# Six of the eight chunks of the output projection moved into the retention stage, their partial sums kept in DRAM

## The chip, the cores and the metric

The kernel runs on one core of one Trainium2 chip. The metric is the device time of one execution in microseconds (us), the median of three runs. All times of instructions come from one profiled execution, counted from the start of its span.

## What is computed

Two layers over 768 tokens (512 latent tokens and 256 context tokens), width 1024, all in float32. Each layer projects the normed input once, feeds the columns to three groups of heads, joins their outputs, multiplies by `w_out`, and then runs a squared-ReLU channel mixer. Cut to what matters here:

```python
def trunk_layer(...):
    h = rmsnorm(x, norm_g[0]) * (1 + sc1) + sh1
    qa, ka, va, qr, kr, vr, gr, z, xbc, dt = split(h @ w_in)
    att = attention_mixer(...)        # 6 heads of 64: features 0..383
    ret = retention_mixer(...)        # 4 heads of 64: features 384..639
    ssd = ssd_mixer(...)              # 6 heads of 64: features 640..1023
    o = concatenate([att, ret, ssd]) @ w_out
    x = x + g1 * rmsnorm(o, norm_g[1])
    h2 = rmsnorm(x, norm_g[2]) * (1 + sc2) + sh2
    x = x + g2 * rmsnorm(square(relu(h2 @ w_ff1)) @ w_ff2, norm_g[3])
```

The context stream goes through the same steps in layer 0 and is not needed after the mixers of layer 1. So layer 0 handles six tiles of 128 tokens, layer 1 four. The adaLN terms (`sh`, `sc`, `g`) are products of two conditioning vectors with `w_mod`, in 12 sections of 512 columns a layer.

## The kernel before

**Products.** A float32 operand is split into two parts, high and low, and every large product is three matmuls (`mm3`, L465): high by high, high by low and low by high. A weight unit (`wunit`, L210) is loaded raw by SP's queue into one of three buffers `wr` (512 KB each), the high part is made by ACT (L221) and the low part by DVE (L222, or POOL), into one of three buffers `wh` and `wl`.

**Order.** The program is written as one stream of instructions; a scheduler at build time gives every engine and SP's queue a fixed order from it. An instruction that stands earlier in the text goes first when both are ready, one that is not ready in the scheduler's reckoning is overtaken. At run time each engine works through its own list in order, and so does SP's queue. Generators are interleaved by hand: `run(gen, n)` takes `n` steps.

**The mixers** (`mixers`, L501) end with attention and retention. While the six attention heads run (L1127), one step of `fill` is taken after each pair of query tiles, three pairs a head in layer 0 and two in layer 1. `fill` (L1124) holds 12 steps in layer 0 and 10 in layer 1 that project the retention's keys, values, queries and gates, and in layer 0 then 24 steps that compute modulation sections 4 to 9: sections 4 and 5 split (`mod_split`), sections 6 to 9 as plain float32 products (`mod_whole`, L320, whose matmul is L325). In layer 0 what is left of `fill` is taken in the retention, five steps at a time.

**Retention** (L1143 to L1161) has four heads. A head transposes its keys and queries (`ret_prep`, L999), multiplies scores (`rs`, L1035) and chunk sums (`rd`, L1039), runs a chain of ten small DVE steps for the states (L1050, L1052), multiplies the outputs (`ry`, L1056 and L1057), and norms them on ACT and DVE (L1064 to L1074). After heads 1 and 3 the finished pair is transposed into chunk 3 and chunk 4 of `mixT` (`put_tok`, L1107; the high part on ACT, L1101, the low part on DVE, L1103). Chunks 0 to 2 (attention) and 5 to 7 (state-space) are put there as well, by `puts`, in heads 0 to 2. The POOL engine multiplies `kw` (L1006) and the gains (L1086, L1087) and makes the low part of chunks 0 to 2 (L1103).

**The output projection** (`wout_phase`, L1192) takes 8 chunks by 2 halves of 512 columns by 3 matmuls for each tile of tokens: 48 matmuls of 128x512. The first six products of tile 0 (18 matmuls) are issued in head 3 of the retention (`wout_begin`, L1180), the rest after it. The chunks go in this order, those of the retention last:

```python
WO_ORDER = [5, 6, 7, 0, 1, 2, 3, 4]
```

Its weights are four units, each four chunks by 512 columns.

**After each tile** `sandwich` (L1219) takes the two halves out of PSUM: ACT squares them (L1230), DVE multiplies them by the gate row (L1232), a root gives the factor, DVE adds the residual (L1236), the sum is stored, and `norm_tile` (L451) norms it again: square (L428), root, scale (L454), eight transposes on PE (`nps`), modulation on DVE and ACT (L445, L443), high part (L448), low part (L449). Its scratch `tt` (`t` in the code, later `xh`) and `xt` have two buffers each; `tt` is in use from the gate multiply to L449. Beside the last tile PE runs the first products of the channel mixer (`ff_begin`, L1253) on tokens whose norm is done; then the channel mixer goes on and needs the last tile's high part first.

**Memory.** The mixers' pool is closed before the pool of the output stage is opened, and the latter may lie in the memory of the former.

## Time and profile before

| | |
|---|---|
| three runs | 1888.5, 1886.2, 1888.09 us |
| median | 1888.09 us |
| profiled execution: span from its first to its last instruction | 1880.8 us |
| PE busy | 1753.1 us, 93% |
| DVE busy | 1219.7 us, 65% |
| ACT busy | 703.0 us, 37% |
| POOL busy | 369.1 us, 20% |
| moved by DMA | 217.00 MB, mean 115 GB/s |

The profile gives the span of the profiled execution; a time of its own beside that span was not recorded. The median of the runs is 7.3 us above the span. PE is TensorE, PEld its weight loads, which run beside the matmuls. A matmul's recorded time reaches over the next one's start, so the step from one start to the next says what it costs PE. PEclk is the granted clock as a share of 2.4 GHz. In a row of the timeline, what stands in brackets is the idle time before the instruction and what ended it.

### The profile page before, as it was taken

Reading aid. Unit: us, or ns where it says so; the run is one execution under the profiler, and the core shown is the slowest. Engines: PE = TensorE matmul, PEld = TensorE weight load, DVE = VectorE, ACT = ScalarE, POOL = GpSimd, SP = SyncE. Lnnn points to the kernel's source line nnn. Section 1 sums busy time; section 2 is a strip of 40 time slices with the busy share of each in tenths; the row PEclk is TensorE's granted clock in tenths of the full one; section 3 lists DMA queues with packets and bytes.
Section 4 is the critical chain, followed back from the end, with each engine's and each line's share of the span. In section 5 each row is a group of like instructions: output and inputs, shape, how many; then the busy total and the mean of one; then the engine's idle time right before and its main releaser. Section 6 shows DMA issues by size and latency. Waiting matters only on the chain. (4 is left out here: it accounts for less than half of the span.)

```text
span 1880.8 us, 24641 instructions
## 1 busy us (share of the span) xinstructions
PE 1753.1 (93%) x8991; PEld 1443.0 (77%) x8991; DVE 1219.7 (65%) x2462; ACT 703.0 (37%) x1267; POOL 369.1 (20%) x391
## 2 busy tenths in 40 slices
PE   6987999997999999999999979888987999999998
PEld 2877977655878888888888868777866788888886
DVE  5868985664668566566566586788876654444445
ACT  5543376652461111201201275433772532222222
POOL 0047232313001100100100132553022021111112
PEclk9999999997999999999999999999996999999999
DMA  8410243366444334434434433224324432222332
GB/s 274 124 52 32 89 149 104 104 182 184 146 135 136 124 101 132 125 107 123 126 105 118 152 123 91 65 71 124 100 73 110 147 122 90 90 90 91 102 105 95
DMA packets 189078, 217.00 MB, mean 115 GB/s; under 512 B 67667, under 2 KB 142237, under 8 KB 188957
## 3 DMA queue, kind: packets, MB, share of 16 engines
q1 hardware_dynamic: 188956, 215.43, 37.8%
q8 instruction: 71, 1.16, 0.2%
q14 instruction: 51, 0.41, 0.1%
HBM read 189.66 MB, written 25.72 MB: 115 GB/s over the span
## 5 line engine op out<-in xcount | busy, mean ns | idle before, releaser
L467 PE MATMUL f<-h_h,wh_f 128*128 128x512 f32 (+1 forms) x800 | 280.3, 351 | 1.4 <-ACT h_h L448 1.4
L469 PE MATMUL f<-h_h,wl_f 128*128 128x512 f32 (+1 forms) x800 | 281.0, 352 | 0.0
L468 PE MATMUL f<-h_l,wh_f 128*128 128x512 f32 (+1 forms) x800 | 280.1, 350 | 0.8 <-DVE h_l L449 0.8
L1299 POOL TENSOR_TENSOR r<-r 128x768 f32<-128x768 f32 (+1 forms) x64 | 93.8, 1466 | 847.4 <-ACT r L1298 837.8
L467 PE MATMUL f<-wh_g,uh 128*128 128x512 f32 x640 | 253.0, 396 | 4.1 <-DVE acc L1327 1.7
L468 PE MATMUL f<-wl_g,uh 128*128 128x512 f32 x640 | 252.6, 395 | 0.0
L469 PE MATMUL f<-wh_g,ul 128*128 128x512 f32 x640 | 251.8, 394 | 0.0
L221 ACT ACTIVATE wh_f<-wr_f 128x1024 fp32r<-128x1024 f32 x64 | 66.5, 1055 | 377.2 <-PE f L469 164.4
L1329 DVE TENSOR_TENSOR acc<-acc,f 128x512 f32<-128x512 f32 x140 | 96.0, 686 | 121.0 <-PE f L469 119.6
L467 PEld LDWEIGHTS f<-h_h,wh_f 128*128 128x128 f32 x800 | 152.0, 190 | 23.0 <-ACT h_h L448 1.5
L468 PEld LDWEIGHTS f<-h_l,wh_f 128*128 128x128 f32 x800 | 151.1, 189 | 22.8 <-DVE h_l L449 1.0
L469 PEld LDWEIGHTS f<-h_h,wl_f 128*128 128x128 f32 x800 | 151.2, 189 | 20.8
L405 DVE SCALAR_TENSOR_TENSOR ga<-wr_mg,cg_a,ga 128x512 f32<-128x512 f32 x216 | 153.6, 762 | 14.6 <-DMA wr_mg<-in_w_mod_dram 14.6
L467 PEld LDWEIGHTS f<-wh_g,uh 128*128 128x128 f32 x640 | 120.1, 188 | 33.5 <-DVE acc L1327 2.2
L469 PEld LDWEIGHTS f<-wh_g,ul 128*128 128x128 f32 x640 | 120.1, 188 | 28.8
L468 PEld LDWEIGHTS f<-wl_g,uh 128*128 128x128 f32 x640 | 120.2, 188 | 27.4 <-DVE wl_g L222 0.2
L1298 ACT ACTIVATE r<-f 128x768 f32<-128x768 f32 (+1 forms) x64 | 44.8, 699 | 193.4 <-PE f L469 133.4
L1300 DVE CAST uh<-r 128x768 fp32r<-128x768 f32 (+1 forms) x64 | 32.3, 505 | 123.2 <-POOL r L1299 123.2
L222 DVE TENSOR_TENSOR wl_f<-wr_f,wh_f 128x1024 fp32r<-128x1024 f32 x64 | 77.6, 1220 | 51.3 <-ACT wh_f L221 51.3
L222 DVE TENSOR_TENSOR wl_g<-wr_g,wh_g 128x1024 fp32r<-128x1024 f32 x62 | 76.6, 1241 | 50.9 <-ACT wh_g L221 50.8
L221 ACT ACTIVATE wh_g<-wr_g 128x1024 fp32r<-128x1024 f32 x64 | 67.3, 1056 | 94.2 <-DMA wr_g<-in_w_ff_dram 53.6
L467 PE MATMUL xbc<-h_h,wh_xbc 128*128 128x512 f32 (+1 forms) x208 | 73.5, 353 | 7.7 <-ACT cin L692 7.7
(405 smaller groups left out, 3774.3 us busy)
## 6 DMA issues: line engine op xcount, KB each, us to landing
wr_f<-in_w_ff_dram SPq DMA_DIRECT2D x64, 512.0 KB, 3.7
wr_g<-in_w_ff_dram SPq DMA_DIRECT2D x64, 512.0 KB, 3.5
wr_mg<-in_w_mod_dram SPq DMA_DIRECT2D x192, 128.0 KB, 2.9
wr_m<-in_w_mod_dram SPq DMA_DIRECT2D x24, 512.0 KB, 3.8
m<-in_w_mod_dram SPq DMA_DIRECT2D x32, 256.0 KB, 4.2
wr_o<-in_w_out_dram SPq DMA_DIRECT2D x16, 512.0 KB, 4.1
wr_xbc<-in_w_in_dram SPq DMA_DIRECT2D x14, 512.0 KB, 5.3
xmid<-xt SPq DMA_DIRECT2D x10, 512.0 KB, 2.6
```

Source lines behind the costliest of these rows:

```text
L221: S.activation(hv[:, a0 : a0 + an], r, AF.Copy)
L222: (lo_eng or V).tensor_tensor(lv[:, a0 : a0 + an], r, hv[:, a0 : a0 + an].bitcast(F32), ALU.subtract)
L405: V.scalar_tensor_tensor(acc[:, s], r2[:, k % 2], w, acc[:, s], ALU.mult, ALU.add)
L467: T.matmul(o, a[0], b[0], start=first, stop=False)
L468: T.matmul(o, a[0], b[1], start=False, stop=False)
L469: T.matmul(o, a[1], b[0], start=False, stop=last)
L1298: S.activation(r, q[:, :NT], AF.Relu)
L1299: G.tensor_tensor(r, r, r, ALU.mult)
L1300: V.tensor_copy(uh, r)
L1329: V.tensor_tensor(acc[tt][:, ns], acc[tt][:, ns], qs[tt][half], ALU.add)
```

## The change

The attention loop takes five steps of `fill` a time in heads 4 and 5, and whatever is left is taken before the retention begins. `wout_begin` now loads three units of two chunks each (chunks 5 and 6, 7 and 0, 1 and 2, all 1024 columns), with the six `puts` in between, ahead of head 0. Then it runs six chunks for every tile and half as a step-wise generator, two steps after each step of a head: a half is 18 matmuls into a PSUM bank, a copy by ACT into a staging buffer, and a store of 256 KB to the DRAM tensor `opd`. A half is two steps, so there are 24 steps in layer 0 and 16 in layer 1. `wout_phase` loads one unit (chunks 3 and 4), runs 12 matmuls a tile, and `sandwich` loads the tile's row block of `opd` into `t`, adds the two halves of PSUM to it on DVE, and goes on from there; the gate multiply moves from DVE to POOL, but for the last tile. Lines of comment that the change takes out are left away here.

```diff
             for _ in att_head(h):
-                run(fill, 1)
+                run(fill, 1 if h < 4 else 5)
+        run(fill)
         mixT = alloc_mix()
...
-        puts = [lambda j=j: put_ssd(j) for j in range(3)] + [lambda j=j: put_att(j) for j in range(3)]
-        wpre = None
-        wo = iter(())
+        wo = wout_begin(l, mixT, stage, [lambda j=j: put_ssd(j) for j in range(3)] + [lambda j=j: put_att(j) for j in range(3)])
+        next(wo)
         for h in range(4):
-            if h == (3, 2)[l] and l in (0,1,):
-                wpre = wout_units(l, (0,))
-            if h == (3, 3)[l] and wpre:
-                wo = wout_begin(l, mixT, wpre, 6)
             if h < 3:
                 ret_decay(h + 1)
                 ret_prep(h + 1)
                 centre_v(h + 1)
             for i, _ in enumerate(ret_head(h)):
-                run(fill, 5)
                 if i == 1:
                     ret_gain(h)
-                if i in (0,2) and puts:
-                    puts.pop(0)()
                 run(wo, 2)
-        run(fill)
         run(wo)
...
+    WO_FIRST = ((5, 6), (7, 0), (1, 2))
+    WO_LAST = (3, 4)
+    opd = [dp.tile([TOK, D], F32, name=f"opd{l}") for l in range(DEPTH)]
+    def wout_unit(l, ks):
+        src = lambda a0, an: [(krows(w_out[l], ks[a0], 1, 0, D), 0, D)]
+        return wunit(src, (128, 2, D), f"o{l}{ks[0]}")
...
+    def wout_begin(l, mixT, stage, puts):
+        NQ = 6 if l < DEPTH - 1 else 4
+        us = []
+        for n, ks in enumerate(WO_FIRST):
+            us.append(wout_unit(l, ks))
+            for _ in ks:
+                puts.pop(0)()
+        yield
+        for tt in range(NQ):
+            cols = slice(tt * 128, (tt + 1) * 128)
+            for half in range(2):
+                q = pB([128, 512], f"ob{l}{tt}{half}")
+                for u, ks in enumerate(WO_FIRST):
+                    for i, k in enumerate(ks):
+                        wout_part(mixT, us[u], q, i, k, cols, half, u + i == 0, u + i == 3)
+                    if u == 1:
+                        yield
+                o = stage(512, f"ob{tt}{half}")
+                S.activation(o, q, AF.Copy)
+                nc.sync.dma_start(rows(opd[l], tt)[:, half * 512 : (half + 1) * 512], o)
+                yield
     def wout_phase(l, cpool, mixT, h2T):
...
+        w = wout_unit(l, WO_LAST)
         for tt in range(NQ):
...
             for half in range(2):
-                d = done[half] if tt == 0 else 0
-                q.append(q0[half] if tt == 0 and q0[0] is not None else (pB, pC)[tt % 2]([128, 512], f"op{l}{half}{tt}"))
-                for i in range(d, KC):
-                    wout_part(mixT, us, q[half], half, WO_ORDER[i], cols, i == 0, i == KC - 1)
+                q.append((pB, pC)[tt % 2]([128, 512], f"op{l}{half}{tt}"))
+                for i, k in enumerate(WO_LAST):
+                    wout_part(mixT, w, q[half], i, k, cols, half, i == 0, i == 1)
...
-            sandwich(cpool, q, g1, x_in(l, tt), rows(xmid[l], tt), tt, l, 1, h2T, V, 2, pC if last else None)
+            sandwich(cpool, q, g1, x_in(l, tt), rows(xmid[l], tt), tt, l, 1, h2T, V, 2, pC if last else None, V if last else G, rows(opd[l], tt))
...
         hv = (slice(0, 512), slice(512, 1024))
+        if part is not None:
+            nc.sync.dma_start(t, part)
+            for j in range(2):
+                V.tensor_tensor(t[:, hv[j]], t[:, hv[j]], o[j], ALU.add)
+            o = [t[:, hv[j]] for j in range(2)]
         for j in range(2):
             S.activation(junk, o[j], AF.Square, accum_out=ss[:, j : j + 1])
```

## Rows read from the trace of the kernel before

**Rows 1.** The page: busy time of each engine.

```profile
PE 1753.1 (93%) x8991; PEld 1443.0 (77%) x8991; DVE 1219.7 (65%) x2462; ACT 703.0 (37%) x1267; POOL 369.1 (20%) x391
```

**Rows 2.** Busy time by stretch: PE, PEld, DVE, ACT, POOL, granted clock, DMA share, GB/s.

```profile
355.00:401.30 46.30, 43.62 (x225) 24.15 (x224) 31.97 (x73) 32.74 (x68) 13.80 (x7) 1.00 0.55 155
...
437.00:491.30 54.30, 44.71 (x250) 39.33 (x251) 36.12 (x94) 17.93 (x25) 13.11 (x12) 0.81 0.47 141
491.30:561.40 70.10, 67.60 (x318) 54.71 (x316) 45.16 (x110) 44.85 (x92) 0.00 (x0) 1.00 0.46 155
1411.60:1471.80 60.20, 48.22 (x242) 42.59 (x241) 40.32 (x132) 15.13 (x29) 13.96 (x14) 0.72 0.34 80
1471.80:1526.50 54.70, 52.50 (x303) 44.91 (x301) 35.72 (x76) 35.02 (x67) 6.62 (x2) 1.00 0.56 192
```

**Rows 3.** The same view, head 1 of layer 1's retention.

```profile
1425.00:1437.90 12.90, 10.84 (x54) 9.82 (x53) 9.17 (x35) 3.64 (x9) 2.72 (x3) 0.63 0.25 67
```

**Rows 4.** PE's timeline: outputs of one retention head in layer 0.

```profile
445.72 0.39 PE L1056 MATMUL ry<-vrr,W 128*128 128x64 f32 x2
445.95 0.39 PE L1057 MATMUL ry<-rst,q 128*128 128x64 f32 x2
...
447.88 0.64 PE L1056 MATMUL ry<-vrr,W 128*128 128x64 f32 x2
448.31 0.63 PE L1057 MATMUL ry<-rst,q 128*128 128x64 f32 x2
```

**Rows 5.** Granted clock around them, columns as in rows 2.

```profile
441.70:447.00 5.30, 2.76 (x24) 2.51 (x22) 3.70 (x10) 1.63 (x2) 3.52 (x3) 1.00 0.98 267
447.40:463.80 16.40, 10.24 (x47) 9.71 (x46) 11.84 (x32) 4.55 (x7) 5.36 (x5) 0.50 0.36 123
```

**Rows 6.** Groups of PE instructions, 401.3 to 491.3 us: busy, mean ns, idle before.

```profile
L325 PE MATMUL mq<-wr_m,csil 128*2 128x512 f32 x42 | 19.6, 592 | 2.2 <-DMA wr_m<-in_w_mod_dram 2.1
L1057 PE MATMUL ry<-rst,q 128*128 128x64 f32 x48 | 11.4, 327 | 8.7 <-DVE rst L1052 8.7
L467 PE MATMUL op<-wh_o,mix_h 128*128 128x512 f32 x24 | 9.8, 409 | 0.0
```

**Rows 7.** PE's timeline: the first and the last of 39 products in a row.

```profile
523.09 0.39 PE L467 MATMUL op<-wh_o,mix_h 128*128 128x512 f32 x1
...
531.87 0.39 PE L469 MATMUL op<-wh_o,mix_l 128*128 128x512 f32 x1
```

**Rows 8.** Last output of head 3 on PE, and chunk 4's low part on DVE.

```profile
482.81 0.39 PE L1057 MATMUL ry<-rst,q 128*128 128x64 f32 x2
...
490.36 0.96 DVE L1103 TENSOR_TENSOR mix_l<-sT,mix_h 128x768 fp32r<-128x768 f32 x1 [2.28 <-ACT mix_h L1101]
...
1464.65 0.39 PE L1057 MATMUL ry<-rst,q 128*128 128x64 f32 x2
...
1471.07 0.69 DVE L1103 TENSOR_TENSOR mix_l<-sT,mix_h 128x512 fp32r<-128x512 f32 x1 [1.63 <-ACT mix_h L1101]
```

**Rows 9.** Last tile of layer 0: second square (ACT) and low part (DVE), timeline.

```profile
546.88 0.58 ACT L1230 ACTIVATE junk<-op 128x512 f32<-128x512 f32 x1
...
561.34 1.23 DVE L449 TENSOR_TENSOR h_l<-tt,h_h 128x1024 fp32r<-128x1024 f32 x1 [1.69 <-ACT h_h L448]
```

**Rows 10.** Loads of `xt`: first issue in layer 0; time to landing, layer 0, then 1.

```profile
490.03 0.90 SPq L1223 DMA_DIRECT2D xt<-in_x_dram  x2
...
DMA to landing us min/median/max: 4.2/5.0/5.4
...
DMA to landing us min/median/max: 2.6/2.6/2.6
```

**Rows 11.** POOL's and DVE's timelines: a small DVE step beside POOL, and without it.

```profile
452.42 1.81 POOL L1103 TENSOR_TENSOR mix_l<-fa,mix_h 128x768 fp32r<-128x768 f32 x1 [1.52 <-ACT mix_h L1101]
...
453.02 1.23 DVE L1069 TENSOR_SCALAR var<-var 128x6 f32<-128x6 f32 x1
...
468.78 0.17 DVE L1069 TENSOR_SCALAR var<-var 128x6 f32<-128x6 f32 x1
```

More of the change, by code (lines that the diff above doesn't have):

```diff
@@ L1153, in mixers @@
             for i, _ in enumerate(ret_head(h)):
-                run(fill, 5)
                 if i == 1:
                     ret_gain(h)
-                if i in (0,2) and puts:
-                    puts.pop(0)()
                 run(wo, 2)
-        run(fill)
         run(wo)
-        return mixT, wpre
-    WO_ORDER = [5, 6, 7, 0, 1, 2, 3, 4]
-    def wout_unit(l, half, u, pool=None):
-        return wunit(wcols(w_out[l], 4 * u, [(half * 512, 0, 512)]), (128, 4, 512), f"o{l}{half}{u}", None, pool)
@@ L1170, in wout_units @@
-    def wout_units(l, halves):
-        us = {(half, u): wout_unit(l, half, u) for half in halves for u in ((1, 0) if half == 0 else (1,))}
-        return us, [None, None], [0, 0]
-    def wout_part(mixT, us, q, half, k, cols, first, last):
-        mh, ml = mixT
-        h, lo = us[half, k // 4]
-        mm3(q, (mh[:, k, cols], ml[:, k, cols]), (h[:, k % 4, :], lo[:, k % 4, :]), first, last)
-    def wout_begin(l, mixT, pre, n):
-        us, q, done = pre
-        for i in range(n):
-            half, j = divmod(i, 6)
-            if i == 0:
-                t = pA([128, 2, 512], f"op{l}0")
-                q[:] = [t[:, 0], t[:, 1]]
-            wout_part(mixT, us, q[half], half, WO_ORDER[j], slice(0, 128), j == 0, False)
-            done[half] = j + 1
-            yield
+        return mixT
@@ new lines, in tile_hybrid_backbone, with wout_part @@
+    WO_FIRST = ((5, 6), (7, 0), (1, 2))
[4 more added lines that the diff above has]
+        return wunit(src, (128, 2, D), f"o{l}{ks[0]}")
+    def wout_part(mixT, w, q, i, k, cols, half, first, last):
+        mh, ml = mixT
+        h, lo = w
+        ns = slice(half * 512, (half + 1) * 512)
+        mm3(q, (mh[:, k, cols], ml[:, k, cols]), (h[:, i, ns], lo[:, i, ns]), first, last)
@@ L1192, in wout_phase @@
     def wout_phase(l, cpool, mixT, h2T):
         NQ = 6 if l < DEPTH - 1 else 4
-        mixT, wpre = mixT
-        us, q0, done = wpre or ({}, [None, None], [0, 0])
-        for half in range(2):
-            for u in (1, 0):
-                if (half, u) not in us:
-                    us[half, u] = wout_unit(l, half, u, cpool if half == 1 and (u == 0 or l == 1) else None)
+        w = wout_unit(l, WO_LAST)
         for tt in range(NQ):
@@ L1217, in wout_phase, with sandwich @@
         return pre
-    def sandwich(pool, o, gate, xsrc, xdst, tt, nl, nwhich, hT, eng, bufs=2, half_bank=None, geng=None):
+    def sandwich(pool, o, gate, xsrc, xdst, tt, nl, nwhich, hT, eng, bufs=2, half_bank=None, geng=None, part=None):
         xt = pool.tile([128, D], F32, tag="xt", name="xt", bufs=bufs)
@@ L1425, in tile_hybrid_backbone @@
         mixT = mixers(0, mp, hT, lambda: big(pa, "mix0"), kvw)
-    dump("mix0", mixT[0][0].bitcast(F32))
+    dump("mix0", mixT[0].bitcast(F32))
     R = ExitStack()
@@ L1441, in tile_hybrid_backbone @@
         mixT = mixers(1, mp, hT, lambda: big(pr, "mix1", SEQ), kvw)
-    dump("mix1", mixT[0][0].bitcast(F32))
+    dump("mix1", mixT[0].bitcast(F32))
     L = ExitStack()
```

## The prediction

> **What bounds the kernel now.** I read the page first. PE is busy for 1753.1 of 1880.8 us [rows 1], so a change pays only by filling PE's gaps or by emptying its list, and this one empties nothing: 288 products in layer 0 and 192 in layer 1 are issued before and after it. Next I cut the span at the stages that the diff touches [rows 2]. In layer 0 they are attention heads 4 and 5 (355.0 to 401.3), retention (to 491.3, when chunk 4 stands in `mixT`) and output projection (to 561.4, when PE goes on with the channel mixer); in layer 1 retention (1411.6 to 1471.8) and output projection (to 1526.5). The reader is to see two kinds of stage. The output stages are dense: PE 67.6 of 70.1 us and 52.5 of 54.7, clock 1.00. The retention stages are not: 44.7 of 54.3 us at clock 0.81 and 48.2 of 60.2 at 0.72. A head without products beside it is worst: head 1 of layer 1 takes 12.9 us at clock 0.63 [rows 3]. Thirdly I asked what PE waits for there: the chain of small DVE steps that makes the states, 8.7 us in layer 0 [rows 6].
>
> The step from one product to the next is (531.87 - 523.09) / 38 = 0.231 us [rows 7], that of a small matmul 0.115 us, and 0.215 us once the granted clock has gone from 1.00 to 0.50 [rows 4, 5].
>
> **The change, part by part.** Every sum is made against the profiled execution. Its span is 1880.8 us; the median of the runs, 1888.1, lies 7.3 above it, and I carry that over.
>
> *Modulation moves ahead of the retention (layer 0).* 42 records of the plain float32 products still run after 401.3 and cost PE 19.6 us [rows 6]. They now stand ahead in the text. Attention has 46.3 - 43.6 = 2.7 us of PE idle to take them [rows 2], so attention ends at 401.3 + 19.6 - 2.7 = 418.2. This is work moved, not saved. Its loads move with it on SP's queue, past the loads of keys and queries of heads 4 and 5; DMA is busy for 0.55 of attention [rows 2], so there is room, and I charge nothing. If that cover fails, the price is the 2.1 us that these records wait for DMA now [rows 6]. In layer 1 `fill` is used up within head 4, and nothing moves.
>
> *Products move into the retention.* 216 in layer 0 and 144 in layer 1, at 0.231 us: 49.9 and 33.3 us. Each step of a head is followed by two of the 24 (16) steps, so layer 0 spends ten in head 0, ten in head 1 and four in head 2; layer 1 spends all in heads 0 and 1. After that no product is left. A head has 63 small matmuls in layer 0 (12 transposes, 12 scores, 12 sums, 24 outputs, 3 for chunks), 46 in layer 1, so 7.2 and 5.3 us at the full clock; the transposes of chunks 5 to 7 add 2.1 and 1.4.
>
> Where products stand behind it, a head's chain is hidden. Where none stand, I price the head by the row of a bare one, 12.9 us [rows 3]: in layer 0 head 3, 5.7 over its matmuls; in layer 1 heads 2 and 3, 7.6 each. Head 2 of layer 0 has 36 products, 8.3 us, over 5.7, and is covered. Then the tail of head 3 is bare as well: from its last output on PE to chunk 4's low part, 483.2 to 491.3 = 8.1 us, and 1465.0 to 1471.8 = 6.7 [rows 8]. The kernel before runs products in both.
>
> The first product needs its weights and chunks 5 and 6. The raw loads are 3.1 MB; at 267 GB/s [rows 5] that is 11.8 us if nothing is loaded early, and nothing if the buffers come free in time. I take 4, nearer the low end, because they stand right behind the modulation's loads.
>
> So chunk 4 stands at 418.2 + 4 x 7.2 + 2.1 + 49.9 + 4 + 5.7 + 8.1 = 516.8 in layer 0, 25.5 later than now, and at 1411.6 + 4 x 5.3 + 1.4 + 33.3 + 4 + 15.2 + 6.7 = 1493.4 in layer 1, 21.6 later.
>
> *Copies and stores of the partial sums.* 20 copies by ACT, at the 0.58 us of a square of the same shape [rows 9], stand beside an ACT that is busy for 17.9 of 54.3 us [rows 2]: hidden. But a bank must be copied before PE may fill it again, and a head's outputs use the same two banks; bounds 0 and one copy each, 20 x 0.58 = 11.6 us. I take 0, since the other bank is mostly free. The 20 stores go on SP's queue at some 0.45 us each [rows 10] with DMA 0.47 and 0.34 busy [rows 2]; behind each stand the next head's loads, for which heads 0 and 1 now leave twice the time. Nothing is charged.
>
> *The last stage thins out.* A tile has 12 products, 2.8 us, where it had 48, 11.1 us. PE no longer sets its pace. What does? ACT and DVE are busy for 44.9 and 45.2 us over six tiles [rows 2], 7.5 us a tile each. But the scratch `tt` has two buffers and is now held from the load of the partial sums to the low part of the normed tile: load 2.6 us as in layer 1 [rows 10], two adds at 0.69 (two inputs of 128x512 on DVE, as chunk 4's low part in layer 1 [rows 8]), then from the second square to the low part 546.9 to 562.6 = 15.7 us in the last tile, the one with least company [rows 9]. That is 19.7 us for two tiles, 9.8 each, over 7.5. Layer 0 has two such cycles before its last pair starts, layer 1 one.
>
> The first loads can't come early: `xt` is first issued at 490.03 [rows 10], when the mixers' memory is free, and lands after 5.0. That was hidden behind PE's many products; now it stands on the path. The pair's second tile starts 3.9 us behind the first (1.05 MB at 267 GB/s). The last tile takes 1.4 + 15.7 = 17.1, of which PE doesn't wait for the last 1.2. Layer 0: 5.0 + 2 x 19.7 + 3.9 + 17.1 - 1.2 = 64.2 against 70.1, so 5.9 won. Layer 1: 5.0 + 19.7 + 3.9 + 17.1 - 1.2 = 44.5 against 54.7, so 10.2 won. The channel mixer's first products lie beside it in both kernels.
>
> *Gate multiply to POOL.* 16 of 20 leave DVE (0.69 us each) for POOL, at some 1.2 us (an estimate: two thirds of the 1.81 that POOL takes for 768 columns [rows 11]). The root's chain beside them is longer, so 0. But one small DVE step takes 1.23 us beside POOL's multiply and 0.17 without it [rows 11], which bounds the loss at two multiplies, 2.4 us, a tile. I take 0 and keep the other end as a rival.
>
> *Sum:* layer 0 +25.5 - 5.9 = +19.6, layer 1 +21.6 - 10.2 = +11.4, together +31. Span 1912, median **1919 us**. In short: 83 us of PE's work goes into stages with about 50 us of gaps, half of it into two heads that can't use it all, and the stage it leaves doesn't shrink by as much, since something else paces it.
>
> One rule is weighed here. The clock falls when PE thins out, 1.00 to 0.50 in rows 5. The Trainium skill, Perfetto Trace Analysis, Matmul Optimizations, says that the matmul engine scales with its utilisation, so matmuls should come back-to-back in batches. The filled heads are counted at the full clock already; in the last stage, by that rule, eight transposes a tile at 0.215 in place of 0.115 would put 0.8 us on each of five chains, 4 us, and the sum would be 1923.
>
> **The rivals.**
>
> *Gaps filled by readiness, faster.* The scheduler may let PE take a head's matmuls first and products only in the gaps, so that they last through head 3. For it: head 3 of layer 0 has 24 products of this form [rows 6] where the text gives it 6; the others were pulled ahead. Against: products stand ahead of the next head's work in the text. It takes away 5.7 + 15.2 = 20.9 us and leaves +10. It decides if the tile's chain is also shorter than 15.7 - 10 / 5 = 13.7 us (three cycles and two last tiles hang on it). ACT and DVE together have 15.0 us of work a tile, weight casts and parallel parts among it, so 12 is possible: 31 - 21 - 18 = -8, 1880 us.
>
> *POOL holds DVE, slower still.* By rows 11 it can: two multiplies of 1.2 a tile, mostly beside the other tile's chain. At 3.5 us a chain, between one tile's 2.4 and the pair's 4.8, five times: +17, 1936 us. Against it: POOL has nothing else to do there. The Trainium skill speaks against the move too: Perfetto Trace Analysis, Optimizing Scalar/DVE Operations, says that the two engines share an SBUF read port, so that offloading between them might not help.
>
> *The change doesn't do what it says.* If weights or chunks come so late that the products run behind the heads, three more heads of layer 0 and two of layer 1 are bare: 3 x 5.7 + 2 x 7.6 = +32, 1951 us. Against it: DMA's free share.
>
> **How the numbers follow.** The forecast has 0.47, POOL 0.18, late products 0.07, all slower. The filled gaps have 0.28; only with the short chain do they win, so 0.22 is faster and 0.06 within 0.2% (3.8 us, about what a measurement can tell from no change). Range: the low end goes to 1876, under the second rival's 1880 by its unknown ends (the 4 us of weights); the high end to 1947, past POOL's 1936 by the copies' 11.6, leaving out most of the late products.
>
> **What would show it.** Right: in heads 0 and 1 products stand between a head's matmuls at clock 1.00; in layer 1 heads 2 and 3 have none and the clock falls; chunk 4 comes some 20 us later in both layers; in the last stage PE idles, `tt` of tile n+2 is loaded right after L449 of tile n, and L449 comes every 10 us. Wrong: products between the outputs of head 3; L449 every 7.5 us; or chunk 4 less than 10 us later.

## The result, and the profile after

The changed kernel takes 1979.4 us (median of four runs, 1975.8 to 1989.9) against 1888.3 for the kernel before beside it: a ratio of 1.049, 95% interval 1.046 to 1.052. Slower was right; 31 us were forecast, and 91 came, above the range's high end of 1947. The profiled execution is the longest of the four: 1989.9 us, span 1988.1, so 107 over the span before. Span is set against span below, and two things have to be kept in mind: this execution lies 10 us over its median, and the one profiled of the kernel before some 6 us under. In every run an execution's time is 1.7 to 2.2 us above its span, so the span of 1880.8 belongs to an execution of about 1882.7 us, where the median is 1888.3; the 7.3 us between median and span that the prediction carries over are in the main this.

The page's engine line shows that no work was saved and little added; PE's list is as long as before, and every engine but PE has room [rows 1]:

```profile
PE 1791.5 (90%) x8991; PEld 1468.2 (74%) x8991; DVE 1232.0 (62%) x2466; ACT 715.9 (36%) x1287; POOL 395.9 (20%) x407
```

Busy time by stretch, columns as in [rows 2]: attention heads 4 and 5, retention and last stage of layer 0; then the end of attention in layer 1, behind `fill`'s last product, its retention and its last stage. A last stage ends here with the last L449:

```profile
355.00:428.90 73.90, 67.97 (x297) 31.39 (x295) 37.42 (x88) 39.61 (x80) 14.51 (x6) 0.97 0.63 187
428.90:544.60 115.70, 101.83 (x501) 84.76 (x501) 59.45 (x145) 34.44 (x50) 22.15 (x19) 0.81 0.48 137
544.60:629.80 85.20, 42.50 (x158) 32.11 (x156) 47.21 (x106) 42.95 (x88) 14.33 (x10) 0.70 0.39 134
...
1460.40:1488.40 28.00, 19.69 (x107) 15.94 (x105) 20.83 (x40) 18.92 (x36) 3.91 (x5) 0.82 0.47 133
...
1488.40:1571.60 83.20, 73.67 (x347) 61.03 (x347) 49.42 (x137) 23.58 (x41) 15.05 (x14) 0.81 0.42 120
1571.60:1628.10 56.50, 29.25 (x150) 25.37 (x150) 30.59 (x71) 28.08 (x58) 13.24 (x8) 0.67 0.44 148
```

The reader is to see that the last stages lost most of their PE work, 42.5 us where 67.6 stood [rows 2], and became longer. Measured to the same mark, the kernel before took 71.2 and 50.0 us for them.

Three places tell why. The first is the start of layer 0's retention, in the timelines of PE and of SP's queue:

```profile
427.77 1.25 PE L961 MATMUL pv<-PT,vat 128*128 128x256 f32 x4 [1.73 <-DVE PT L957]
432.71 1.51 PE L152 MATMUL dTkr<-ident,ddkr 128*128 128x128 f32 x6 [3.68 <-DMA ddkr<-krd]
436.53 1.51 PE L152 MATMUL dTqr<-ident,ddqr 128*128 128x128 f32 x6 [2.31 <-DMA ddqr<-qrd]
...
448.72 0.77 PE L468 MATMUL ob<-wl_o,mix_h 128*128 128x512 f32 x1
```

```profile
432.01 0.45 SPq L966 DMA_DIRECT2D attd<-fo  x1
432.50 1.21 SPq L1004 DMA_DIRECT2D ddqr<-qrd  x2
```

Head 0's queries are loaded behind attention's last store, which waits for attention's last copy. The head's scores (L1035) begin at 439.8, 10.8 us after attention, and the moved products in earnest at 448.7, 20 us after it. In the kernel before, the loads of head 0's queries stand ahead of attention's last store (SP's queue), and its transposes and scores (PE) begin within 2.4 us of attention's end:

```profile
396.39 0.58 SPq L1004 DMA_DIRECT2D ddqr<-qrd  x1
...
402.67 0.46 SPq L966 DMA_DIRECT2D attd<-fo  x1
```

```profile
401.31 0.82 PE L152 MATMUL dTqr<-ident,ddqr 128*128 128x128 f32 x6
402.06 1.88 PE L325 MATMUL mq<-wr_m,csil 128*2 128x512 f32 x4
403.87 1.60 PE L1035 MATMUL rs<-qT,kT 64*128 64x128 f32 x12
```

The modulation's products [rows 6] ran there between the matmuls of heads 0 and 1, from 402.1 to 435.8.

The second is the cycle of the last stage: L449 of tiles 0, 2 and 4, the loads of the partial sums (SP), and the start of tile 2 on DVE beside POOL's gate multiply:

```profile
568.00 1.23 DVE L449 TENSOR_TENSOR h_l<-tt,h_h 128x1024 fp32r<-128x1024 f32 x1 [3.04 <-ACT h_h L448]
...
591.04 1.23 DVE L449 TENSOR_TENSOR h_l<-tt,h_h 128x1024 fp32r<-128x1024 f32 x1 [0.88 <-ACT h_h L448]
...
617.24 1.23 DVE L449 TENSOR_TENSOR h_l<-tt,h_h 128x1024 fp32r<-128x1024 f32 x1 [2.81 <-ACT h_h L448]
```

```profile
569.29 7.16 SPq L1228 DMA_DIRECT2D tt<-opd  x2
```

```profile
573.64 1.28 DVE L1230 TENSOR_TENSOR tt<-tt,op 128x512 f32<-128x512 f32 x2 [3.13 <-DMA tt<-opd]
...
575.98 1.24 DVE L1236 TENSOR_TENSOR oss<-oss 128x1 f32<-128x1 f32 x1
```

```profile
575.22 3.22 POOL L1235 TENSOR_TENSOR tt<-tt,gr 128x512 f32<-128x512 f32 x2 [15.75 <-ACT junk L1233]
```

The load of tile 2 is issued when tile 0's L449 is done (569.29), and the adds start 4.4 us later. From one pair's L449 to the next it is 23.0 and 26.2 us.

The third is the last tile: PE's and DVE's timelines.

```profile
624.80 1.04 PE L152 MATMUL nps<-ident,tt 128*128 128x128 f32 x8
```

```profile
625.44 1.37 DVE L445 TENSOR_SCALAR tt<-nps,abc 128x128 f32<-128x128 f32 x4 [6.97 <-PE nps L152]
```

Its scaled rows (L454) stand at 615.10 + 1.16 = 616.3, but PE is at `ff_begin`'s 48 products, 611.86 to 624.56, which come first in its list: 8.5 us lost. In the kernel before the same 48 products end at 557.6, when the last tile's scaled rows have stood for half a microsecond (ACT, then PE):

```profile
555.92 1.14 ACT L454 ACTIVATE tt<-xt,nrs 128x1024 f32<-128x1024 f32 x1
```

```profile
557.58 1.03 PE L152 MATMUL nps<-ident,tt 128*128 128x128 f32 x8
```

### The profile page after: what moved, and what is told of

Same layout as the page of the kernel before. It is cut to its first block, busy times and chain, and to the rows that moved or that the text cites. A ratio compares the mean times of both kernels' runs of the same rounds, so it can differ in the third digit from the quotient of the medians.

```text
span 1988.1 us, 24778 instructions
## 1 busy us (share of the span) xinstructions
PE 1791.5 (90%) x8991; PEld 1468.2 (74%) x8991; DVE 1232.0 (62%) x2466; ACT 715.9 (36%) x1287; POOL 395.9 (20%) x407
## 3 DMA queue, kind: packets, MB, share of 16 engines
q8 instruction: 71, 1.16, 0.2%
```

## The experiments

Fifteen kernels were run, each against the kernel before on the same chip. This table has the lengths of those on which the text rests, in their profiled executions and to 0.2 us, all from the starts and ends of the same instructions: last `pv` product (L961), chunk 4's low part (L1103), last L449 of a stage. "Tail 1" is attention in layer 1 behind `fill`'s last product.

| kernel | attention 0 ends | retention 0 | last stage 0 | tail 1 | retention 1 | last stage 1 | span |
|---|---|---|---|---|---|---|---|
| before | 401.5 | 89.9 | 71.2 | 19.2 | 60.2 | 50.0 | 1880.8 |
| after | 428.9 | 115.7 | 85.2 | 28.0 | 83.2 | 56.5 | 1988.1 |
| e1 | 429.1 | 110.7 | 84.5 | 26.6 | 83.1 | 57.2 | 1975.3 |
| e2 | 428.9 | 110.2 | 70.7 | 29.9 | 76.8 | 48.1 | 1945.0 |
| e3 | 403.4 | 130.6 | 83.7 | 21.1 | 85.6 | 56.1 | 1972.1 |
| e4 | 425.9 | 97.2 | 96.8 | 29.8 | 68.3 | 54.8 | 1957.5 |
| e5 | 404.2 | 122.9 | 57.5 | 20.4 | 72.7 | 47.3 | 1924.3 |
| e7 | 401.5 | 105.6 | 74.4 | 21.1 | 60.2 | 52.5 | 1906.0 |
| e9 | 425.6 | 82.0 | 77.4 | 25.5 | 64.8 | 56.0 | 1915.4 |
| e10 | 429.1 | 115.1 | 63.1 | 30.0 | 83.8 | 43.1 | 1954.3 |
| e13 | 400.4 | 129.7 | 75.9 | 20.3 | 72.9 | 46.6 | 1931.9 |
| e15 | 401.7 | 94.0 | 71.2 | 20.7 | 64.5 | 53.9 | 1892.4 |

Each row is one execution, and one stage of it can be some 5 us longer or shorter for no reason in the program. The kernel before and e15 run the same instructions in the same order on every engine through all of layer 0, and its retention took 89.8 us in one and 94.0 in the other; the granted clock was 0.89 and 0.84:

```profile
401.50:491.30 89.80, 76.46 (x397) 52.98 (x396) 55.34 (x153) 26.76 (x42) 18.33 (x18) 0.89 0.61 176
```

```profile
401.70:495.70 94.00, 81.03 (x397) 56.82 (x396) 55.46 (x154) 26.77 (x42) 18.32 (x18) 0.84 0.58 169
```

The changed kernel, e1, e2 and e10 too have one order up to the last stage of layer 0, and their retentions there took 115.7, 110.7, 110.2 and 115.1. Two marks need care. "Tail 1" grows when `fill` ends earlier, though attention need not end later: from layer 1's first `xbc` product to the end of its attention it is 279.6 us before, 288.2 in the changed kernel, 281.7 in e1 and 281.8 in e9. And the last L449 of a stage comes early where its transposes stand ahead of `ff_begin`'s products, as in e5, whose products then still have to be done behind it.

The scheduler at build time pulls products of the output projection ahead, so that more stand in the retention than the text gives it. These ran ahead of chunk 4's low part in the kernel before (tile `op`), in layer 0 and then in layer 1:

```profile
401.50:491.31 89.81, 17.44 (x70) 12.82 (x71) 0.00 (x0) 0.00 (x0) 0.89 0.61 176
1411.60:1471.76 60.16, 12.34 (x49) 8.76 (x49) 0.00 (x0) 0.00 (x0) 0.72 0.34 80
```

So 70 and 49 of 288 and 192 products stood there already, where the text has 18. The changed kernel has 230 and 158 (216 and 144 moved, and 14 of chunk 3 in either layer): its retentions took in 160 and 109 products, 37.0 and 25.2 us at 0.231 each, and its last stages lost as many. The expectations of e7, e11, e13 and e15 count from 18.

### e1: the gate multiply back on DVE

```diff
-            sandwich(cpool, q, g1, x_in(l, tt), rows(xmid[l], tt), tt, l, 1, h2T, V, 2, pC if last else None, V if last else G, rows(opd[l], tt))
+            sandwich(cpool, q, g1, x_in(l, tt), rows(xmid[l], tt), tt, l, 1, h2T, V, 2, pC if last else None, V, rows(opd[l], tt))
```

> Edit: the gate multiply of all tiles of the output stage back on DVE; nothing else. Base is the changed kernel, 1979.4 us. Theory A (what paces the output stage is the cycle of the two-buffer scratch tt: load of the partial sums, adds, chain, low part; POOL is a side matter): the multiply takes 0.69 instead of 1.28 to 1.98 us and the small DVE steps beside it 0.15 instead of 1.2, at most some 1.5 us a tile of which 8 in 10 lie on the cycle: 1967 to 1976. Rival B (POOL holds DVE, the 17 us of the prediction's rival and more, since the stage came out 35 us longer than forecast in both layers): 1955 or less. If DVE becomes the bound instead: 1980 or more.

Measured: 1979.8 us (1975.6 to 1984.9). Neither A's small gain nor B's large one: the last stages are as long as with POOL (84.5 and 57.2). Its profiled execution lies within 3 us of its median, so up to the gate multiply its stages are the better measure of the changed kernel's.

### e2: a tile of its own for the load, three buffers for `xt` and `tt`

```diff
-            sandwich(cpool, q, g1, x_in(l, tt), rows(xmid[l], tt), tt, l, 1, h2T, V, 2, pC if last else None, V if last else G, rows(opd[l], tt))
+            sandwich(cpool, q, g1, x_in(l, tt), rows(xmid[l], tt), tt, l, 1, h2T, V, 3, pC if last else None, V if last else G, rows(opd[l], tt))
...
-            nc.sync.dma_start(t, part)
+            p = pool.tile([128, D], F32, tag="pt", name="pt", bufs=2)
+            nc.sync.dma_start(p, part)
             for j in range(2):
-                V.tensor_tensor(t[:, hv[j]], t[:, hv[j]], o[j], ALU.add)
-            o = [t[:, hv[j]] for j in range(2)]
+                V.tensor_tensor(p[:, hv[j]], p[:, hv[j]], o[j], ALU.add)
+            o = [p[:, hv[j]] for j in range(2)]
```

> Edit: the partial sums are loaded into a tile of their own (two buffers) and xt and tt get three buffers; gate multiply stays on POOL. Theory A (two-buffer cycle): loads of tiles 2 to 5 no longer wait for L449 of two tiles back, so some 4.3 us of load and 3 to 6 us of chain leave each of two cycles in layer 0 and one in layer 1: 1979.4 - 3 x 9 = 1952, between 1940 and 1965. Rival B (POOL and the chain of a tile itself pace it, whatever the buffers): 1972 or more.

Measured: 1949.3 us (1946.8 to 1954.3), ratio 1.033 (1.029 to 1.036). Theory A, and 30 of 91 us. The last stages fall to 70.7 and 48.1, 22.9 us together. L449 of tiles 0, 2 and 4 now, 15.7 and 17.0 us apart:

```profile
563.75 1.23 DVE L449 TENSOR_TENSOR h_l<-tt,h_h 128x1024 fp32r<-128x1024 f32 x1 [0.39 <-ACT h_h L448]
...
579.44 1.22 DVE L449 TENSOR_TENSOR h_l<-tt,h_h 128x1024 fp32r<-128x1024 f32 x1 [2.15 <-ACT h_h L448]
...
596.40 1.23 DVE L449 TENSOR_TENSOR h_l<-tt,h_h 128x1024 fp32r<-128x1024 f32 x1 [2.75 <-ACT h_h L448]
```

Layer 1's retention is 6 us shorter here too, which the edit doesn't explain and which is little more than one execution's play.

### e3: the modulation behind the retention's first loads

```diff
-                run(fill, 1 if h < 4 else 5)
-        run(fill)
+                run(fill, 1)
...
         centre_v(0)
+        run(fill)
```

> Edit: in attention one step of fill follows each step again, as in the kernel before; what is left of the modulation is issued right behind the loads of retention head 0 instead of ahead of them. Theory C (the modulation's products were the cover of the retention's first loads: PE now idles from 428.6 to 439.8 us for keys and queries queued behind attention's last store on SP, and in layer 1 head 5 of attention is bare since fill was used up in head 4): 10 us come back in layer 0 and 4 in layer 1, 1965, between 1958 and 1972. Rival D (the place of these products doesn't matter; the retention is paced by its own products and the weights): 1976 to 1983.

Measured: 1969.1 us (1958.2 to 1973.8), ratio 1.041 (1.036 to 1.045). Theory C's total. Attention and retention of layer 0 end at 534.0 (after: 544.6, e1: 539.8), 10.6 or 5.8 us earlier. The 4 us of layer 1 aren't seen: its tail goes from 28.0 to 21.1, but from the first `xbc` product to the end of attention it is 282.5 us, where e1 has 281.7. And the edit does two things at once: it puts the modulation behind head 0's loads, and with that these loads ahead of attention's last store again (the transposes of its queries at 403.2, before attention's end at 403.4). Which of the two gives the time back is not shown.

### e4: one step of products instead of two

```diff
-                run(wo, 2)
+                run(wo, 1)
```

> Edit: one step of the moved products instead of two behind each step of a retention head, so that 20 of 24 (layer 0) and 16 of 16 (layer 1) are spread over all four heads. Theory E (the prediction's: heads without products are bare, 5.7 us in layer 0's head 3 and 7.6 each in heads 2 and 3 of layer 1): up to 5.7 + 15.2 = 21 us come back, 1960, between 1955 and 1968. Rival F (a head's chain isn't covered by 9 products, and the bank each holds across a step delays the head's outputs): 1972 or more.

Measured: 1960.8 us (1959.3 to 1967.8), ratio 1.039 (1.036 to 1.042): theory E, 19 us. Its retentions, layer 0 and then layer 1:

```profile
425.90:523.10 97.20, 86.39 (x469) 70.99 (x469) 53.45 (x139) 26.21 (x41) 21.25 (x19) 0.92 0.43 123
...
1474.70:1543.00 68.30, 61.44 (x348) 50.45 (x348) 48.17 (x137) 24.22 (x41) 14.43 (x14) 0.98 0.46 131
```

Layer 1, where the steps last to the end of head 3, gains 14.9 us and the clock 0.98. Layer 0 gains 18.5 us (13.5 against e1) and gives 11.6 (12.3) back in the last stage. There 18 of the moved products and 14 of chunk 3 now run behind chunk 4, 32 in all or 7.4 us, where e5's expectation says 36.

### e5: the three together; e6: the stores from ACT's queue

e5 is e2 and e3 with the following, and e6 is e5 with the stores of `opd` issued by ACT.

```diff
-                run(wo, 2)
+                run(wo, 2 if wc and i == 0 else 1)
```

> Edit: runs e2 and e3 together, and the products spread over the heads so that none is left behind head 3 (two steps behind the first step of a head in layer 0, one behind each other, six a head). Theory: the three losses lie in different stages and add up: 1979.4 - 30 (load tile) - 10 (modulation) - 19 (spread), and up to 8 more, since in e4 the 36 products left behind chunk 4 lengthened the output stage by 11.6: 1912 to 1922. It stays above the kernel before, since the output stage keeps its 70 us, paced by the tiles' own chains, though PE has little to do there. Rival G (the losses are one shared resource, DMA or ACT and DVE work, so that they don't add): 1930 or more.

> Edit: e5, and the stores of the partial sums are issued by ACT, right behind their copies, instead of by SP. Theory H (SP waits up to 10 and 18 us at a time for copies, with the next head's keys and queries queued behind, and that delays heads): 5 us or more under e5. Rival (PE has other products in that time, so that these waits cost nothing, as the prediction charged): within 3 us of e5.

Measured: e5 1926.7 us (1925.1 to 1928.7), ratio 1.020 (1.019 to 1.022); e6 1932.2 (1930.3 to 1935.4). The losses add up nearly (53 of 59), which falls between the theory's range and rival G's. Theory H falls: e6 is 5.5 us slower, so SP's waits for the copies, up to 9.1 us at a time in the changed kernel, cost nothing that can be won back like this. (The 10 and 18 us of the expectation are rows of SP's timeline with three and four stores taken together.) 38 us remain. These are e5's retention and last stage in layer 0, then the same in layer 1:

```profile
404.20:527.10 122.90, 112.36 (x558) 80.63 (x556) 60.53 (x158) 37.94 (x57) 20.55 (x18) 0.95 0.57 172
527.10:584.60 57.50, 32.30 (x121) 23.99 (x120) 45.34 (x108) 40.70 (x87) 13.51 (x10) 0.69 0.63 217
1445.90:1518.60 72.70, 65.43 (x352) 54.33 (x352) 48.35 (x138) 24.52 (x42) 14.25 (x14) 0.93 0.45 126
1518.60:1565.90 47.30, 30.57 (x159) 26.01 (x159) 30.55 (x71) 27.91 (x58) 13.18 (x8) 0.71 0.55 197
```

The retentions are filled, PE busy for 112.4 of 122.9 us and 65.4 of 72.7, and they grew by 33.0 and 12.5, for 160 and 110 products more, 37.0 and 25.4 us: in layer 0 nearly all of them lengthened it, in layer 1 half. The last stages gave back 13.7 and 2.7, and the first of these not in full: L449 ends earlier, but in layer 0 the channel mixer's first high part comes 14.5 us behind it (584.6 to 599.1), where it came 7.0 behind it before.

### e7 and e8: only the first tiles moved

Two tiles of each layer, and three in layer 0; the others are computed whole in the last stage.

```diff
-        for tt in range(NQ):
+        for tt in range(NMOVE[l]):
...
-                run(wo, 2)
+                run(wo, 1 if i < 2 else 0)
```

> Edit: only the first two tiles of each layer get their six chunks ahead, two steps a head; the other four (layer 1: two) are computed whole in the last stage, dense as before; modulation as in e3, gate multiply on DVE. Theory I (a product pays in the retention only as long as it falls into a gap, and in the last stage only as long as the stage isn't left to the tiles' chains): 72 products, 16.6 us, go into gaps in either layer, and the last stage shrinks with them by 5 to 10: 1865 to 1885, faster than the kernel before. Rival J (what is won in the last stage is lost in the retention whatever the amount): 1885 to 1905.

> Edit: e7 with three tiles moved in layer 0 (three steps a head), still two in layer 1. Theory I: the third tile's 36 products no longer find gaps, and layer 0's last stage begins to thin out: 0 to 8 us above e7. Rival (gaps still open): 3 us or more under e7.

Measured: e7 1907.7 us, ratio 1.011 (1.009 to 1.013); e8 1919.5, 1.016 (1.015 to 1.018), 12 us above e7, past theory I's 8. Less moved is less lost, but theory I falls, since e7 is slower than the kernel before. These are the moved products (`ob`) in e7's retentions, to be set beside the 70 and 49 above; no whole product of tile `op` runs there:

```profile
401.50:507.10 105.60, 25.58 (x72) 15.38 (x72) 2.39 (x4) 0.82 0.54 161
1435.00:1495.30 60.30, 21.94 (x72) 14.74 (x72) 2.39 (x4) 0.80 0.38 94
```

In layer 0 that is 2 products more than before, and the retention is 15.7 us longer. What differs there is not how many products stand in it but where. The modulation runs in one block ahead of head 0's scores, which begin at 430.2 (28.7 us after attention, 2.4 before), the products are spread over the four heads, and none is left for head 3's outputs and tail (491.9 to 507.1), which had products beside them before. In layer 1 the retention takes 23 more in its 60.2 us, and yet its last stage, with 23 fewer, goes from 50.0 to 52.5, which is within one execution's play.

### e9: the kernel before, with the change's pacing of `fill` alone

```diff
-                run(fill, 1)
+                run(fill, 1 if h < 4 else 5)
+        run(fill)
```

> Edit: the kernel before, with the change's pacing of fill alone (five steps behind each step of attention heads 4 and 5, the rest ahead of the retention; no product of the output projection is moved). Theory C (these records filled the gaps at the start of the retention; ahead of it they stand beside nothing, and layer 1's head 5 goes bare): e3 gave back 10 of the change's 91 us, so 6 to 15 us above the kernel before. Rival D (work moved, not lost, as the prediction had it): within 4 us of it.

Measured: 1917.5 us (1911.9 to 1921.1), ratio 1.014 (1.012 to 1.017): 28 us, twice what theory C gave it. Attention ends 24.1 us later, and the retention behind it is only 7.9 us shorter: here too head 0's queries are loaded behind attention's last store, and the scores begin 8.9 us after attention, 6.5 later than before. Layer 1's tail is 6.3 us longer, but from the first `xbc` product to the end of its attention only 2.2 are lost. In stages whose text is untouched, this execution is longer by 6.2 us in layer 0's last stage, by 4.6 in layer 1's retention and by 6.0 in its last stage; against a profiled execution of the kernel before that is itself 6 us under its median, single differences of this size are at the edge of what can be told. In one place, though, a changed order is seen. This is layer 1's last stage on DVE's timeline, then on POOL's:

```profile
1531.18 0.16 DVE L175 RECIPROCAL ors<-rm_t 128x1 f32<-128x1 f32 x1
1531.25 1.20 DVE L222 TENSOR_TENSOR wl_f<-wr_f,wh_f 128x1024 fp32r<-128x1024 f32 x1
1532.37 0.21 DVE L177 SCALAR_TENSOR_TENSOR rm_t<-ors,rm_h 128x1 f32<-128x1 f32 x1
1532.50 1.22 DVE L222 TENSOR_TENSOR wl_f<-wr_f,wh_f 128x1024 fp32r<-128x1024 f32 x1
1533.64 2.39 DVE L181 SCALAR_TENSOR_TENSOR ors<-rm_t,ors 128x1 f32<-128x1 f32 x1
```

```profile
1533.61 2.39 POOL L222 TENSOR_TENSOR wl_g<-wr_g,wh_g 128x1024 fp32r<-128x1024 f32 x1 [54.78 <-ACT wh_g L221]
```

The root's chain of tile 2 has two weight casts inside it, and its last step lies beside a cast on POOL: from reciprocal to factor 4.85 us. In the kernel before (DVE's timeline of the same tile) the two casts stand behind the chain, which takes 0.61 us:

```profile
1497.84 0.16 DVE L175 RECIPROCAL ors<-rm_t 128x1 f32<-128x1 f32 x1
1498.04 0.22 DVE L177 SCALAR_TENSOR_TENSOR rm_t<-ors,rm_h 128x1 f32<-128x1 f32 x1
1498.29 0.16 DVE L181 SCALAR_TENSOR_TENSOR ors<-rm_t,ors 128x1 f32<-128x1 f32 x1
...
1503.62 2.35 DVE L222 TENSOR_TENSOR wl_f<-wr_f,wh_f 128x1024 fp32r<-128x1024 f32 x2
```

### e10: the last stage without the partial sums

```diff
-            sandwich(cpool, q, g1, x_in(l, tt), rows(xmid[l], tt), tt, l, 1, h2T, V, 2, pC if last else None, V if last else G, rows(opd[l], tt))
+            sandwich(cpool, q, g1, x_in(l, tt), rows(xmid[l], tt), tt, l, 1, h2T, V, 2, pC if last else None, V)
```

> Edit: the changed kernel with the last stage's load and addition of the partial sums left out (so chunks 5 to 2 are missing in its output), and the gate multiply on DVE, as PSUM is read again; all products, copies and stores stay. What remains in the last stage is 12 products a tile and the tile's chain, two buffers. Theory K (the tiles' chains on ACT and DVE pace the last stage in both kernels; the many products of the kernel before lay hidden beside them): layer 0's last stage, 71.2 us before and 84.5 in e1, comes to 60 to 72, total 1945 to 1965. Rival (the load and the adds cost all of the difference to the forecast and more; without them the stage falls to the 45 us that ACT and DVE are busy): 1935 or less.

Measured: 1941.4 us (1939.5 to 1956.2), ratio 1.028 (1.025 to 1.031). Both last stages:

```profile
544.20:607.30 63.10, 38.31 (x158) 30.09 (x156) 39.27 (x104) 41.08 (x88) 0.00 (x0) 0.77 0.38 130
1551.70:1594.80 43.10, 26.36 (x150) 23.03 (x149) 26.95 (x68) 27.20 (x58) 4.70 (x2) 0.73 0.41 145
```

With a quarter of the products and no partial sums to load, the stages take 63.1 and 43.1 us, where they took 71.2 and 50.0 with 218 and 143 products and e1 had 84.5 and 57.2. That is theory K for the stage, by its own number; the total came a little under K's 1945. The profiled execution is the longest of the five, 15 us over the median; its excess over e1 shows in layer 0's retention (115.1 against 110.7) and in layer 1's mixers (287.6 us from the first `xbc` product to the end of attention, against 281.7), so the last stages may be read.

### e11 and e12: fewer tiles, modulation in its old place

e11 moves one tile in layer 0 (in head 3) and two in layer 1, and starts the last stage with a tile that isn't moved; e12 moves none in layer 0.

```diff
-        for tt in range(NQ):
+        for turn, tt in enumerate((n, *range(n), *range(n + 1, NQ))):
```

> Edit: modulation and puts in their old places; layer 0 moves one tile, in head 3; layer 1 moves two, two steps a head; the last stage starts with a tile that is not moved, so that its six first chunks stand behind head 3's tail as in the kernel before and cover the loads. Theory I in its milder form (e7's layer 1 took 54 more products than the kernel before in the same 60.2 us; what it lost was the tail and the start of the last stage): 1875 to 1889. Rival (the last stage is paced by its chains, so that it gives nothing back for products taken out of it): 1889 to 1900.

> Edit: e11 with no tile moved in layer 0. Theory I: 0 to 6 us above e11. Rival: the same as e11 or less, since layer 0's gaps are taken by the modulation already.

Measured: 1906.9 us, ratio 1.009 (1.007 to 1.011), and 1911.2, ratio 1.011 (1.008 to 1.013). Theory I's milder form falls, and e11 lies above its rival's range as well; e12's 4.3 us over e11 are within the 0 to 6 that theory I gave it, but the two ranges of runs overlap (1901.8 to 1911.2, 1903.0 to 1914.5). e12 moves no product in layer 0, and yet its retention there takes 103.9 us (before: 89.9), with 56 products ahead of chunk 4; its weight units have another shape and come, with the rest of `fill`, ahead of head 3. Which of these costs it was not run. In layer 1 of e11 the channel mixer's first high part comes 16.1 us behind the last L449 (1535.1 to 1551.2), where it came 5.8 behind it before (1521.9 to 1527.7): the new order puts tile 1 late, and `ff_begin` needs it.

### e13, e14: the modulation in its gaps; e15: half tiles in layer 1

e13 is e5 with the next edit, and in layer 0 `wout_begin` is called at head 2. e14 is e13 with e1's edit. e15 is the kernel before with six chunks of the first half of tiles 1 to 3 of layer 1 computed in heads 2 and 3.

```diff
             for i, _ in enumerate(ret_head(h)):
+                run(fill, 5)
...
-                run(wo, 2 if wc and i == 0 else 1)
+                run(wo, (3 if i < 4 else 0) if wc else 1)
```

> Edit: e5, but in layer 0 the modulation stays where the kernel before has it, five steps behind each step of heads 0 and 1, and the moved products follow in heads 2 and 3 only, three steps behind each of the first four steps of a head. Theory L (e5 is still 38 us above the kernel before because its modulation stands in one block ahead of the heads, where it covers loads but no gaps; e9 puts 28 us on that): 1926.7 - 12 or more, 1900 to 1915. Rival M (the moved products themselves cost it: 46 us of them in layer 0 and 29 in layer 1 went into retentions that grew by 33 and 12.5, and the last stages gave back only 6 and 3): 1919 to 1935.

> Edit: e13 with the gate multiply of all tiles on DVE. Without the two-buffer cycle the tiles' own chains pace the last stage, so POOL's hold on DVE, which cost nothing in e1, should now be seen. Rival B: 6 to 17 us under e13. If DVE is the busier engine by then: e13 or above.

> Edit: the kernel before, with one thing of the change in layer 1 alone: the first half (512 columns) of tiles 1 to 3 gets its six chunks in heads 2 and 3 (54 products, 12.5 us, in place of tile 0's 18), kept in DRAM and added in the last stage from a tile of its own; no further weights are needed for it. Theory I: heads 2 and 3 have room for them and the last stage gives back a few us: 1880 to 1888. Rival M (the last stage is paced by the tiles' chains and gives nothing back): 1888 to 1900.

Measured: e13 1934.2 us (1932.4 to 1935.8), ratio 1.024 (1.022 to 1.027), e14 1931.4 (1926.7 to 1933.0), e15 1893.7, ratio 1.0028 (1.0012 to 1.0044). Rival M by the totals of e13 and e15: with the modulation back in its place e13's retention of layer 0 is 39.8 us longer than before, for 155 products more (225 against 70), 35.8 us. POOL has no price that these runs can tell: e14 is 2.8 us under e13, less than rival B's 6, and the runs of the two overlap. e15 moves 54 products and has 81 ahead of chunk 4 in layer 1 where there were 49. By the medians it is 5.3 us slower, and nothing is given back that can be seen. Where the 5.3 us go can't be read from the traces: the one of e15 is 11.6 us longer, 4.3 in layer 1's retention and 3.9 in its last stage, but also 4.1 in layer 0's retention, which is the same program. No version that was run beats the kernel before.

## Why the prediction was wrong

The direction and the place of the costs were right: more in the retention than the last stage gives back. Each step against the span before, with e1's figure where the changed kernel's execution differs:

- **Modulation moves** (418.2; no charge beyond that). Attention ended at 428.9 (e9: 425.6). "Work moved, not saved" was the step that failed. e9 shows the pacing alone at 28 us: of 24.1 us by which attention grew, the retention gave back 7.9. Two things changed there. The records had run between the matmuls of heads 0 and 1, and those gaps now stand open; and head 0's queries, which had been transposed by attention's end, now come behind attention's last store, so that the scores begin 10.8 us after attention (e9: 8.9) and not 2.4. No run parts the two. "In layer 1 nothing moves" failed as well, by less than the tail says: `fill` ended earlier against attention, whose tail went from 19.2 to 28.0 us; the net loss up to attention's end is 8.6 us in this execution and 2.1 in e1.
- **Retention** (98.6 and 81.8 us). Measured 115.7 and 83.2 (e1: 110.7 and 83.1). Layer 1 was right to 1.4 us, with 14 products of chunk 3, 3.2 us, pulled ahead of chunk 4 that the sum didn't have. In layer 0, the products, once they ran, came every 0.23 us, as said; the 4 us for the first weights and chunks were too few, since the products began in earnest 20 us behind attention, with the clock at 0.50, the 1.2 GHz level, in the middle of that time:

```profile
432.00:446.60 14.60, 11.26 (x45) 9.25 (x46) 9.29 (x19) 4.51 (x7) 2.96 (x2) 0.50 0.86 265
```

- **Bare heads** (5.7 + 15.2). About right: in e4 layer 1's retention is 14.9 us shorter and its clock 0.98; layer 0's is 13.5 shorter than e1's, of which 7.4 are the 32 products that run behind chunk 4, so 6.1 for the 5.7.
- **Copies, stores, SP's waits** (0). Right for SP's waits: e6 is no faster than e5. Copies and stores were not left out in any run.
- **Last stage** (5.9 and 10.2 us won). Measured 14.0 and 6.5 us lost, the largest miss: 20 and 17 us. This is the step that failed most. The mechanism (two buffers of `tt`, load, adds, chain) was right, and e2 takes 22.9 us out of the two stages by undoing it, but its terms were small. A cycle was to take 19.7 and took 23.0 and 26.2 (e1: 23.8 and 23.4). e10, with the gate multiply on DVE as in e1 but no load and no adds, has 16.3 and 17.5 (L449 at 561.2, 577.6 and 595.0), near the 15.7 of the chain; so load and adds cost some 6 to 7.5 where 4.0 were charged. The last tile was to come 3.9 us behind its pair and came 11.3 behind, with 8.5 us of waiting for `ff_begin`'s products in front of its transposes, which hardly waited for them in the kernel before. "The channel mixer's first products lie beside it in both kernels" was the failed sentence.
- **Clock** (4 us, not in the sum). The direction was right: 0.70 and 0.67 in the last stages, and a tile's eight transposes take 1.94 us, where the last tile's, right behind `ff_begin`'s products, take 1.04:

```profile
592.20 1.94 PE L152 MATMUL nps<-ident,tt 128*128 128x128 f32 x8 [6.17 <-ACT tt L454]
```

- **The reading above all this.** I took 67.6 of 70.1 us busy to mean that PE alone sets the pace there ("PE no longer sets its pace", of the stage after), and then expected a stage without that work to be shorter. e10 shows that the 160 and 109 products that left the stages were worth 8.1 and 6.9 us of them, though they are 37.0 and 25.2 us of PE. Most of them had lain beside the tiles' chains. The sum's "83 us of PE's work goes into stages with about 50 us of gaps" was wrong in the same way: 27 us of the 83 stood in the retentions already. The Trainium skill, Perfetto Trace Analysis, Identifying the Most-Contended Engine, says that the matmul's busy share is not a good measure of how close a kernel is to roofline, because pipelined instructions look smaller in the trace. No run here shows that; what they show is that the share says nothing of a second limit: 67.6 of 70.1 us busy, and 63.1 us with a quarter of the products.
- **Rivals.** POOL holding DVE (0.18) fell: single steps are held, 1.24 us for one column beside POOL's multiply, but e1 is level with the changed kernel and e14 within 3 us of e13. Gaps filled (0.28): e4 shows that the spreading it hoped for is worth 19 us, but the change didn't do it. Late products (0.07) were partly there, as the 20 us at layer 0's start.

Together: 76 us of miss from span to span, of which attention in both layers makes 19.3, layer 0's retention 17.1, the last stages 36.6. By the medians the miss is 60 us, and e1's trace, 63 us over the forecast's span, is the better account of it: attention 13.1, layer 0's retention 12.1, the last stages 36.4. What remains open: why stages whose text is the same moved by 6 us in e9 (a changed order was seen in one place, the casts inside the root's chain), and why e13, which undoes the pacing, the two-buffer cycle and the early end of the products, is still 46 us over the kernel before. Rival M puts that down to the moved products themselves; no run leaves them out of the retention alone, so this is argued and not shown.

The Trainium skill, Perfetto Trace Analysis, Identifying Performance Opportunities, Optimization Strategy, says that the same gap repeating on an engine can mean too little space for the next tile, so too few buffers. e2 agrees: with a third buffer and a tile for the load, 23.0 and 26.2 us between pairs became 15.7 and 17.0.

## What to carry to other kernels

A stage in which one engine is dense may have a second limit just below the first; before work is moved out of it, leave that work out in one run and see how far the stage falls. Before products are counted as moved, count in the trace where they run now: here the scheduler had 70 of 288 in the retention where the text had 18. Filler between the parts of a stage full of waits can be worth more than its own time: moved to a dense stage it cost there in full, and most of its gaps stayed; such a move can also change what stands ahead of the next stage's loads. Products that are to fill gaps have to be spread so that some are left for the last gap, and a load into a scratch tile belongs in a tile of its own.

## What the runs showed of the hardware that was not expected

- A DVE step on a single column took 2.39 us, start and end within 0.03 us of a 2.39 us cast on POOL (e9); [rows 11] had 1.23 beside 1.81. Such steps cost a chain where they happen, but putting a whole multiply back on DVE gave nothing.
- The same instructions in the same order on every engine took 89.8 us in one execution and 94.0 in another, with PE's granted clock at 0.89 and 0.84 (layer 0's retention, kernel before and e15). A difference of some 5 us in one stage of two traces says little by itself.
- PE's granted clock follows the gaps closely enough to be seen in a retention: 0.81 in layer 1 of the changed kernel (and of e1), 0.98 with the same products spread (e4), 0.60 in e9, whose retention there has 46 products, all in head 3:

```profile
1435.00:1499.80 64.80, 52.25 (x236) 46.30 (x234) 43.74 (x132) 15.35 (x29) 14.25 (x14) 0.60 0.30 73
```
